# Three of four quads of gate/up as seven products, with one weight sum made by an adding transfer

## The chip, the cores and the metric

The kernel runs on one core of a Trainium2 chip. The metric is the device time of one execution in microseconds (us); the runs shown are three timed executions, and a separate profiled execution gives the trace.

## The reference

Two decoder layers over 256 tokens with 2048 features, all in float32. In each layer a mixer of two head groups (sparse attention with an indexer that picks 64 keys per query, and latent attention) is followed by a layer norm; then comes the part that this change is about:

```python
def _swiglu(x, w_gate, w_up, w_down):
    h = jax.nn.silu(jnp.einsum('bsd,df->bsf', x, w_gate)) * jnp.einsum('bsd,df->bsf', x, w_up)
    return jnp.einsum('bsf,fd->bsd', h, w_down)
...
        x = _layer_norm(ALPHA * x + mix, ln1_g[i], ln1_b[i])
        ffn = _swiglu(x, w_gate[i], w_up[i], w_down[i])
        x = _layer_norm(ALPHA * x + ffn, ln2_g[i], ln2_b[i])
```

The hidden width is 5632.

## The kernel before, in words

**Precision and units.** Every float32 operand of a large matmul is held as two parts, a rounded part (`xh`, `wh`) and the rest (`xl`, `wl`), and a product is three matmuls: high by high, high by low, low by high. Weights come in units: a DMA on the SP queue loads 512 KB into a `raw` tile (128 partitions by 2 k-tiles of 512 columns, line 302); `parts` makes `wh` from it on ScalarE (line 313) and `wl = raw - wh` on VectorE (line 314), both 1024 wide. This is called a split here. There are four `raw` slots, and two more in the phase "more", which holds the output projection's end and the feed-forward stage. For `wh` and `wl` there are five slots each (`UNITS`) and two more in that phase (`MORE`).

**Feed-forward stage.** The 5632 hidden columns are cut into eleven blocks (fc 0 to 10) of 512. A block computes gate and up for two token halves (128 tokens each): four sums over 16 k-tiles. Block 0 does this directly (`gu`). Blocks 1 to 10 (`gate_up`, line 863) treat it as 2 by 2 matrices: token half by contraction half on one side, contraction half by gate/up on the other. A *quad* is the four weight units w11 (gate, unit u), w21 (gate, unit u+4), w12 and w22 (up, the same units). A *plain* quad (`plain_quad`) multiplies all eight pairs. A *seven-product* quad (`wino_quad`, line 905) forms sums of the four weight tiles on VectorE (line 911, four of them, 1024 wide), splits the seven resulting operands, and multiplies them with the tokens or with sums of token tiles (`sum_operands`, kept in the tile `many`) in seven products, each into its own PSUM bank or added onto one of them. After the block's last seven-product quad the banks are recombined on VectorE into gate and up (lines 926 to 959); these statements stand under `tc.high_priority(offset=60)`, which moves them ahead of others that are ready.

The order of quads in each of blocks 1 to 10 is plain, seven-product, plain, seven-product (`ORDER`, line 1023). Behind a block, `hidden` (line 842) takes silu(gate) times up, and three units later transposes the result on PE (line 355) and splits it into `hT`.

**Down.** `down` (line 980) multiplies a pair of hidden blocks with `w_down` for given columns; a half is two of the four column groups, 8 units, 96 matmuls. From block 2 on, half a down pass runs behind the first quad of each block (`behind_quad`, line 1012). For the first pair of blocks VectorE adds it onto the residual `x`, scaled by ALPHA (line 991); for others ScalarE copies it out (line 994) and a DMA issued by GpSimd adds it onto `x` (line 995, `x<-d`, 256 KB). The second half of the last pair and block 10's own part (`last_pass`, line 778) come after block 10; then the last norm (`moments`, line 364, and `norm_out`) writes the output.

**Order.** A planner puts the instructions of each engine and DMA queue into one fixed order ahead of the run, by the program's order and by when it expects an instruction to be ready. An engine works through its order and waits where a value or a buffer isn't there yet.

Of the kernel before, what the change touches and what calls it, by code (L numbers as in the profile page):

```python
# [31 lines left out]
P = 128  # L32
D = 2048
# [23 lines left out]
UNITS, MORE = 5, 2  # L57
# [3 lines left out]
T2 = 11  # L61
# [17 lines left out]
def hybrid_trunk(ctx: ExitStack, tc: tile.TileContext, x, xt_in, pos, w_in, g_cq, g_ckv, w_uq,  # L79
# [34 lines left out]
    def t2(shape, s, dt=F32):  # L114
        return sb.tile(shape, dt, name=nm(s), tag="t2", bufs=T2)

# [70 lines left out]
    def rope_tables():  # L187
        n = NT * NF
        invf = const.tile([P, NF], F32, name="invf")
# [7 lines left out]
        a = const.tile([P, NT, NF], F32, name="ang")  # L197
# [3 lines left out]
        k = const.tile([P, n], F32, name="rk")  # L201
        kh = const.tile([P, n], F32, name="rkh")
# [31 lines left out]
        ab = const.tile([P, NT, NF], F32, name="absang")  # L234
# [86 lines left out]
    def proj(units, lhs, n, before=None, split_t=None):  # L321
# [3 lines left out]
        o = [acc() for _ in range(NT)]  # L325
# [38 lines left out]
    def moments(y):  # L364
# [8 lines left out]
        nc.gpsimd.tensor_scalar(ve, mv[:, 1:2], LN_EPS, None, ALU.add)  # L373
# [41 lines left out]
    def affine(g, b, c):  # L415

        sl = slice(c * C, (c + 1) * C)
        gc, bc = load_gb(g, b, sl)
        for t in range(NT):
            nc.vector.tensor_tensor(xt[t][:, sl], xt[t][:, sl], gc, op=ALU.mult)  # L420
            nc.vector.tensor_tensor(xt[t][:, sl], xt[t][:, sl], bc, op=ALU.add)

    def norm_out(t, gb, m):
        mu, rs = m
        nb = small([P, 1], "bnnb")
        nc.vector.scalar_tensor_tensor(nb, mu, -1.0, rs, op0=ALU.mult, op1=ALU.mult)
        for c in range(D // C):
            sl = slice(c * C, (c + 1) * C)
            y = xt[t][:, sl]
            if t and c == 0:  # L430
                nc.vector.tensor_scalar(y, y, mu, rs, ALU.subtract, ALU.mult)
            else:
                nc.scalar.activation(y, y, AF.Identity, bias=nb, scale=rs)
            nc.vector.tensor_tensor(y, y, gb[c][0], op=ALU.mult)
            (nc.vector if t and c != 1 else nc.gpsimd).tensor_tensor(y, y, gb[c][1], op=ALU.add)
            nc.sync.dma_start(out[t * P:(t + 1) * P, sl], y)
# [43 lines left out]
    def layer(l, xh, xl, norms, last):  # L480
# [297 lines left out]
        def last_pass(unit, ks, lhs, then):  # L778
# [6 lines left out]
            for t in range(NT):  # L785
                for c in range(D // C):
# [10 lines left out]
                    nc.vector.tensor_tensor(sl, sl, o, op=ALU.add)  # L797
# [22 lines left out]
        def sum_operands():  # L820


            for k0, n, where in ((4, 4, many([P, 4, 2, 4, P])),):
                a = {}
                for t in range(NT):
                    for i in range(2):
                        ks = slice(k0 + i * NKT // 2, k0 + i * NKT // 2 + n)
                        v = a[t, i] = t2([P, n, P], "av")
                        nc.vector.tensor_tensor(v, f(xh[t][:, ks, :]), f(xl[t][:, ks, :]), op=ALU.add)
                prev = {}  # L830
                for i, (x, y) in enumerate((((1, 0), (1, 1)), ((0, 0), "s1"), ((1, 0), (0, 0)), ((0, 1), "s2"))):
                    v = prev[f"s{i + 1}"] = t2([P, n, P], "sv")
                    nc.vector.tensor_tensor(v, a[x], prev[y] if isinstance(y, str) else a[y], op=ALU.subtract)
                    hi, lo = where[:, i, 0], where[:, i, 1]
                    split(hi, lo, v)
                    for k in range(n):
                        sums[f"s{i + 1}", k0 + k] = hi[:, k, :], lo[:, k, :]

# [3 lines left out]
        def hidden(gs, us, hT, tr):  # L842

            ss = []
            for t in range(NT):
                g, u = gs[t], us[t]
                s = t2([P, C], "silu")
                nc.scalar.activation(s, g, AF.Silu)
                nc.vector.tensor_tensor(s, s, u, op=ALU.mult)
                ss.append(s)  # L850
            yield 3
            for t in range(NT):
                tp = tr(t)
                transpose4([ss[t][:, j * P:(j + 1) * P] for j in range(4)], tp)
# [250 lines left out]
```

## Time and profile before

| | |
|---|---|
| runs shown | 2196.02, 2196.47, 2197.36 us (median 2196.47) |
| the profiled execution | 2193.86 us, of which its span is 2191.9 us |
| loads of w_gate, w_up, w_down | 176 each, 512 KB each |
| seven-product quads | 40 (160 weight sums on line 911) |
| adding transfers `x<-d` | 64 of 256 KB |

All times of the trace are counted from the start of the span. PE is TensorE's matmuls, PEld its weight loads, DVE is VectorE, ACT ScalarE, POOL GpSimd, SP the engine that issues the loads. In the groups of instructions a row has line, engine, operation, output and inputs with their shapes, count; then busy us in total, mean ns of one; then the engine's idle time before them and who ended it. In a timeline row the first number is the start, the second the duration; brackets give the idle time before it and its end's cause.

### The profile page before, as it was taken

How to read it: one execution, taken by the hardware profiler on the slowest of the kernel's cores; microseconds unless marked ns; L12 is line 12 of the kernel's file. 1: busy time of each engine (PE TensorE's matmuls, PEld its weight loads, DVE VectorE, ACT ScalarE, POOL GpSimd, SP SyncE). 2: the span in 40 equal slices, each digit the busy share in tenths (PEclk: the TensorE clock that was granted, in tenths of full speed). 3: DMA queues.
4: the chain of work that ended last, by engine and by line, in shares of the span. 5: the costliest groups of instructions: out<-in, count | busy, mean ns of one | idle time of the engine just before them, and what ended most of it. 6: DMA issues, size and time to landing. Idle time of an engine off the chain costs nothing. (4 is left out here: it accounts for less than half of the span.)

```text
span 2191.9 us, 27923 instructions
## 1 busy us (share of the span) xinstructions
PE 2169.4 (99%) x10128; PEld 1804.3 (82%) x10128; DVE 1709.0 (78%) x2223; ACT 1196.7 (55%) x1537; POOL 103.9 (5%) x198
## 2 busy tenths in 40 slices
PE   8999999999999999999999999999999999999997
PEld 7888888888888888888888888888888888888886
DVE  6685557989878888887857757678989778888876
ACT  5555554655555555555555554446555655555553
POOL 0100000100000000000001000000000000000012
PEclk9999999999999999999999999999999999999999
DMA  8554456556567667666745455555565667667674
GB/s 299 168 168 154 154 182 210 194 187 216 189 199 245 194 220 240 206 214 203 233 148 170 155 176 178 199 195 186 208 225 183 216 202 231 201 214 238 218 225 133
DMA packets 126058, 437.04 MB, mean 199 GB/s; under 512 B 14320, under 2 KB 14368, under 8 KB 125664
## 3 DMA queue, kind: packets, MB, share of 16 engines
q1 hardware_dynamic: 113760, 409.26, 55.2%
q0 software_dynamic: 12160, 26.01, 6.0%
q8 instruction: 79, 1.29, 0.2%
q14 instruction: 59, 0.48, 0.1%
HBM read 416.33 MB, written 2.10 MB: 191 GB/s over the span
## 5 line engine op out<-in xcount | busy, mean ns | idle before, releaser
L313 ACT ACTIVATE wh<-raw 128x1024 fp32r<-128x1024 f32 (+1 forms) x876 | 916.2, 1056 | 792.2 <-PE acc L337 350.4
L314 DVE TENSOR_TENSOR wl<-raw,wh 128x1024 fp32r<-128x1024 f32 (+1 forms) x876 | 1050.6, 1216 | 379.8 <-ACT wh L313 368.0
L335 PE MATMUL acc<-wh,xh 128*128 128x512 f32 (+1 forms) x768 | 303.4, 396 | 5.9 <-ACT wh L313 5.9
L337 PE MATMUL acc<-wh,xl 128*128 128x512 f32 (+1 forms) x768 | 298.1, 389 | 0.0
L336 PE MATMUL acc<-wl,xh 128*128 128x512 f32 (+1 forms) x768 | 297.5, 388 | 0.0
L335 PE MATMUL acc<-wh,hT 128*128 128x512 f32 x640 | 248.9, 389 | 1.6 <-DVE e L958 1.6
L336 PE MATMUL acc<-wl,hT 128*128 128x512 f32 x640 | 249.0, 389 | 0.0
L337 PE MATMUL acc<-wh,hT 128*128 128x512 f32 x640 | 248.8, 389 | 0.0
L911 DVE TENSOR_TENSOR raw<-raw,raw 128x1024 f32<-128x1024 f32 x160 | 195.7, 1224 | 21.9 <-DMA raw<-in_w_up_dram 17.9
L882 PE MATMUL gu_c<-wh,xl 128*128 128x512 f32 x480 | 186.7, 389 | 0.0
L879 PE MATMUL gu_c<-wh,xh 128*128 128x512 f32 x480 | 186.7, 389 | 0.0
L881 PE MATMUL gu_c<-wl,xh 128*128 128x512 f32 x480 | 186.7, 389 | 0.0
L335 PEld LDWEIGHTS acc<-wh,xh 128*128 128x128 f32 x768 | 144.9, 189 | 36.9 <-ACT wh L313 6.6
L337 PEld LDWEIGHTS acc<-wh,xl 128*128 128x128 f32 x768 | 144.8, 188 | 29.0 <-DVE xl L401 1.0
L336 PEld LDWEIGHTS acc<-wl,xh 128*128 128x128 f32 x768 | 145.1, 189 | 27.6 <-DVE wl L314 1.8
L335 PEld LDWEIGHTS acc<-wh,hT 128*128 128x128 f32 x640 | 120.1, 188 | 27.0 <-DVE e L958 2.0
L337 PEld LDWEIGHTS acc<-wh,hT 128*128 128x128 f32 x640 | 120.1, 188 | 24.9
L336 PEld LDWEIGHTS acc<-wl,hT 128*128 128x128 f32 x640 | 120.2, 188 | 24.8
L879 PE MATMUL att<-wh,xh 128*128 128x512 f32 x320 | 126.1, 394 | 0.0
L882 PE MATMUL att<-wh,xl 128*128 128x512 f32 x320 | 124.9, 390 | 0.0
L881 PE MATMUL att<-wl,xh 128*128 128x512 f32 x320 | 124.6, 389 | 0.0
L995 POOL DMA_DIRECT2D x<-d x64 | 55.1, 879 | 1202.0 <-ACT d L994 697.0
(269 smaller groups left out, 3067.9 us busy)
## 6 DMA issues: line engine op xcount, KB each, us to landing
raw<-in_w_gate_dram SPq DMA_DIRECT2D x176, 512.0 KB, 5.1
raw<-in_w_up_dram SPq DMA_DIRECT2D x176, 512.0 KB, 4.7
raw<-in_w_down_dram SPq DMA_DIRECT2D x176, 512.0 KB, 4.5
raw<-in_w_in_dram SPq DMA_DIRECT2D x144, 512.0 KB, 3.7
raw<-in_w_o_dram SPq DMA_DIRECT2D x64, 512.0 KB, 4.0
x<-d POOLq DMA_DIRECT2D x64, 256.0 KB, 5.8
raw<-in_w_in_dram SPq DMA_DIRECT2D x16, 400.0 KB, 3.1
raw<-in_w_uq_dram SPq DMA_DIRECT2D x12, 512.0 KB, 3.3
```

The source lines that it names most:

```text
L313: nc.scalar.activation(wh[:, :n], raw[:, :n], AF.Copy)
L314: nc.vector.tensor_tensor(wl[:, :n], raw[:, :n], f(wh[:, :n]), op=ALU.subtract)
L335: mm(o[t][:, :n], h, a, start=first, stop=False)
L336: mm(o[t][:, :n], h, b, start=False, stop=False)
L337: mm(o[t][:, :n], l, a, start=False, stop=final)
L879: mm(o[name], h, a, start=name not in begun, stop=False)
L881: mm(o[name], h, b, start=False, stop=False)
L882: mm(o[name], l, a, start=False, stop=end)
L911: nc.vector.tensor_tensor(d, x, y, op=ADD)
L995: nc.gpsimd.dma_start(sl, d, accum_op=ALU.add)
```

## The change

- Blocks 3 to 10 take three of their four quads as seven products, in the order seven-product (unit 1), seven-product (2), plain (0), seven-product (3). Block 1 has three plain quads and one seven-product quad, block 2 keeps two and two. Token sums for unit 1 are added (`few`).
- From block 3 on, the half down pass runs ahead of the block's first quad, and the transposes of the hidden block ahead of it come after eight units, behind that half. The down pass of the last pair is done whole after block 10.
- In a seven-product quad the sum w12 + w22 is made by a DMA: w12 is loaded, and a transfer issued by GpSimd adds w22 onto it from memory; w22 is loaded by itself too. The order of products is p1, p2, p6, p7, p4, p5, p3, and VectorE makes three sums.
- Gate and up, and the two recombined halves, lie in one tile each for both token halves, so that p5, the up bank pair and the product with silu(gate) are each one operation of 1024 for both.
- `MORE` goes from 2 to 3. The temporaries `t2` go from 11 to 5, with 6 more in the attention phase; the rope tables use one of them.
- All down parts go through ScalarE and the adding DMA; ALPHA is put into the gains and offsets of the norm ahead (`affine`, scaled on ScalarE).
- The last norm uses whole gain and offset tiles (three of 1 MB, loaded once gate/up has left their slots); its epsilon step is on VectorE, two of its columns have the offset added by a DMA onto it, no addition is on GpSimd, and the last column is stored in two halves. The additions onto `x` in the last pass are put ahead by 200 (`SOON`).

```diff
-UNITS, MORE = 5, 2
+UNITS, MORE = 5, 3
+SOON = 200
+FIRSTD = 3
-T2 = 11
+T2, T2MORE = 5, 6
...
-        nc.gpsimd.tensor_scalar(ve, mv[:, 1:2], LN_EPS, None, ALU.add)
+        nc.vector.tensor_scalar(ve, mv[:, 1:2], LN_EPS, None, ALU.add)
...
+    def gains():
+
+        g, b, b2 = (t8([P, D], F32, s) for s in ("gall", "ball", "ball"))
+        for d, v in ((g, ln2_g), (b, ln2_b), (b2, ln2_b)):
+            nc.gpsimd.dma_start(d, v[DEPTH - 1].partition_broadcast(P))
+        return g, b, b2
...
             if t and c == 0:
-                nc.vector.tensor_scalar(y, y, mu, rs, ALU.subtract, ALU.mult)
-            else:
-                nc.scalar.activation(y, y, AF.Identity, bias=nb, scale=rs)
-            nc.vector.tensor_tensor(y, y, gb[c][0], op=ALU.mult)
-            (nc.vector if t and c != 1 else nc.gpsimd).tensor_tensor(y, y, gb[c][1], op=ALU.add)
-            nc.sync.dma_start(out[t * P:(t + 1) * P, sl], y)
+                nc.vector.scalar_tensor_tensor(y, y, mu, g[:, sl], op0=ALU.subtract, op1=ALU.mult)
+                nc.vector.scalar_tensor_tensor(y, y, rs, b[:, sl], op0=ALU.mult, op1=ALU.add)
+                store(y, c * C, C)
+                continue
+            nc.scalar.activation(y, y, AF.Identity, bias=nb, scale=rs)
+            nc.vector.tensor_tensor(y, y, g[:, sl], op=ALU.mult)
+            if not t and c < 2:
+                nc.gpsimd.dma_start(b2[:, sl], y, accum_op=ALU.add)
+                late.append(c)
+                continue
+            halves = 2 if t and c == D // C - 1 else 1
...
-            for k0, n, where in ((4, 4, many([P, 4, 2, 4, P])),):
+            few = t8([P, 4, 2, 2, P], F32R, "few")
+            for k0, n, where in ((4, 4, many([P, 4, 2, 4, P])), (2, 2, few)):
...
             def wino_quad(u, final):
-                r11, r21, r12, r22 = (load_raw(w_gu[i][l, fc, v], KU * C) for i, v in
-                                      ((0, u), (0, u + HALF), (1, u), (1, u + HALF)))
+                r12 = load_raw(w_gu[1][l, fc, u], KU * C)
+                nc.gpsimd.dma_start(r12, w_gu[1][l, fc, u + HALF], accum_op=ADD)
+                r11, r21, r22 = (load_raw(w_gu[i][l, fc, v], KU * C) for i, v in ((0, u), (0, u + HALF), (1, u + HALF)))
...
                 p("p2", token(0), r21, hi_)
...
-                add(r11, r11, r12)
-                p("p5", slhs("s1"), r11, lo_)
-                add(r12, r12, r22)
-                add(r11, r11, r22)
+                nc.vector.tensor_tensor(r11, r12, r11, op=ADD)
                 p("p6", slhs("s2"), r11, lo_)
                 if final:
-                    with sooner():
-                        nc.vector.tensor_tensor(e, o["p6"], e, op=ALU.subtract)
+                    on(e[:, 0, :], o["p6"], e[:, 0, :], SUB)
+                nc.vector.tensor_tensor(r21, r11, r21, op=ADD)
+                p("p7", slhs("s3"), r12, lo_)
+                if final:
+                    on(e[:, 1, :], e[:, 0, :], o["p7"], ADD)
                 tick()
-                p("p7", slhs("s3"), r12, lo_)
-                add(r21, r11, r21)
...
                 p("p4", token(1), r21, hi_)
                 if final:
-                    with sooner():
-                        g1 = t2([P, C], "g1")
-                        nc.vector.tensor_tensor(g1, o["c21"], v, op=ALU.subtract)
+                    on(g[:, 1, :], o["c21"], e[:, 1, :], SUB)
+                nc.vector.tensor_tensor(r11, r11, r22, op=SUB)
+                p("p5", slhs("s1"), r11, lo_)
+                if final:
+                    on(e, e, o["p5"].unsqueeze(1).to_broadcast([P, NT, C]), ADD)
                 tick()
                 p("p3", slhs("s4"), r22, lo_)
                 if final:
-                    nc.vector.tensor_tensor(v, v, o["p5"], op=ADD)
-                    nc.vector.tensor_tensor(v, v, o["c22"], op=ADD)
-                    nc.vector.tensor_tensor(e, e, o["p5"], op=ADD)
-                    nc.vector.tensor_tensor(e, e, o["c12"], op=ADD)
+                    on(e, e, o["up"], ADD)
...
                 for t in range(NT):
-                    sl = xt[t][:, c * C:(c + 1) * C]
-                    if fcs[0] == 0:
-                        nc.vector.scalar_tensor_tensor(sl, sl, ALPHA, o[t], op0=ALU.mult, op1=ALU.add)
-                    else:
-                        d = t2([P, C], "d")
-                        nc.scalar.activation(d, o[t], AF.Copy)
-                        nc.gpsimd.dma_start(sl, d, accum_op=ALU.add)
+                    d = t2([P, C], "d")
+                    nc.scalar.activation(d, o[t], AF.Copy)
+                    nc.gpsimd.dma_start(xt[t][:, c * C:(c + 1) * C], d, accum_op=ALU.add)
...
-        ORDER = [("plain", 0), ("wino", 2), ("plain", 1), ("wino", 3)]
+        ORDER = {1: "NNNS", 2: "NSNS"}
+        UNIT = {"NNNS": (0, 1, 2, 3), "NSNS": (0, 2, 1, 3), "SSNS": (1, 2, 0, 3)}
...
         for fc in range(1, NFC):
-            g, u = gate_up(fc, ORDER, behind_quad(fc))
+            order = ORDER.get(fc, "SSNS")
+            if fc >= FIRSTD:
+                down_half(fc)
+                finish_hidden()
+            g, u = gate_up(fc, [({"N": "plain", "S": "wino"}[k], v) for k, v in zip(order, UNIT[order])],
+                           finish_hidden if fc < FIRSTD else None)
...
-        down(held[:2], (2, 3))
+        down(held[:2], range(D // C))
```

More of the change, by code (lines that the diff above doesn't have):

```diff
@@ L319, in load_unit, with proj @@
         return parts(load_raw(src, n), n)
-    def proj(units, lhs, n, before=None, split_t=None):
-        o = [acc() for _ in range(NT)]
+    def proj(units, lhs, n, before=None, split_t=None, banks=None):
+        o = [bank(i, "acc") for i in banks] if banks else [acc() for _ in range(NT)]
         loaded = []
@@ L421, in affine, with store @@
             nc.vector.tensor_tensor(xt[t][:, sl], xt[t][:, sl], bc, op=ALU.add)
+    def gains():
[3 more added lines that the diff above has]
+        return g, b, b2
     def norm_out(t, gb, m):
         mu, rs = m
+        g, b, b2 = gb
         nb = small([P, 1], "bnnb")
         nc.vector.scalar_tensor_tensor(nb, mu, -1.0, rs, op0=ALU.mult, op1=ALU.mult)
+        def store(v, c0, n, queue=nc.sync):
+            queue.dma_start(out[t * P:(t + 1) * P, c0:c0 + n], v)
+        late = []
         for c in range(D // C):
@@ L796, in last_pass @@
                     sl = xt[t][:, c * C:(c + 1) * C]
-                    nc.vector.tensor_tensor(sl, sl, o, op=ALU.add)
+                    with tc.high_priority(offset=SOON):
+                        nc.vector.tensor_tensor(sl, sl, o, op=ALU.add)
                 then(t)
@@ L969, in gate_up @@
                     r = wino_quad(u, i == len(order) - 1)
-                if i == 0:
+                if i == 0 and between:
                     between()
@@ L1003, in layer, with spawn_hidden @@
         held = []
-        def spawn_hidden(fc, g, u, tr):
+        def spawn_hidden(fc, g, u):
             hT = t8([P, 2, 4, S], F32R, "hT")
-            held.append((fc, hT, spawn(hidden(g, u, hT, tr))))
-        def free_banks(t):
-            return bank(2 + t, "tr")
-        def behind_quad(fc):
-            def go():
-                if fc < 2:
-                    return finish(*[h[2] for h in held])
-                down(held[:2], (0, 1) if fc % 2 == 0 else (2, 3))
-                if fc % 2:
-                    del held[:2]
-                finish(*[h[2] for h in held])
-            return go
@@ L1023, in layer, with down_half, finish_hidden @@
-        ORDER = [("plain", 0), ("wino", 2), ("plain", 1), ("wino", 3)]
+            wait = 3 if fc + 1 < FIRSTD else 8 if fc + 1 < NFC else 6
+            held.append((fc, hT, spawn(hidden(g, u, hT, wait))))
+        def down_half(fc):
+            down(held[:2], (0, 1) if fc % 2 else (2, 3))
+            if fc % 2 == 0:
+                del held[:2]
+        def finish_hidden():
+            finish(*[h[2] for h in held])
+        ORDER = {1: "NNNS", 2: "NSNS"}
+        UNIT = {"NNNS": (0, 1, 2, 3), "NSNS": (0, 2, 1, 3), "SSNS": (1, 2, 0, 3)}
@@ L1037, in layer @@
         xh, xl, norms, ms = [], [], [], []
         if last:
-            gb = [load_gb(ln2_g[l], ln2_b[l], slice(c * C, (c + 1) * C)) for c in range(D // C)]
+            gb = gains()
         else:
             gbT = load_gbT(ln2_T[l])
-        down(held[:2], (2, 3))
+        down(held[:2], range(D // C))
         finish(held[2][2])
+        turns["acc"] = 1
         u0 = C // P // KU * (NFC - 1)
```

121 lines of the change are left out of this document (67 added, 54 removed).

## The prediction

> **What bounds the kernel now.** I read the page first (engine totals, clock), then the busy time by stage, then each engine's timeline inside one repeating feed-forward block, then the DMA rows and the last 15 us.
>
> ```profile
> span 2191.9 us, 27923 instructions
> PE 2169.4 (99%) x10128; PEld 1804.3 (82%) x10128; DVE 1709.0 (78%) x2223; ACT 1196.7 (55%) x1537; POOL 103.9 (5%) x198
> PEclk9999999999999999999999999999999999999999
> 1696.50:1759.96 63.46, 63.46 (x286) 52.65 (x285) 52.18 (x51) 36.21 (x39) 3.49 (x4) 1.00 0.68 216
> 2077.26:2142.58 65.32, 63.75 (x286) 52.57 (x285) 52.01 (x51) 36.68 (x40) 7.78 (x12) 1.00 0.75 237
> ```
>
> The first three lines are the page's: TensorE is busy 99% of the span at full clock. The last two are the stage view, for one block (from one pair of hidden transposes to the next) and for the last block: length, then busy time of PE, weight load, DVE, ACT and POOL, the clock, the DMA share, GB/s. In the ordinary block PE is never idle, and VectorE works 52.18 of 63.46 us. A busy PE need not run at its peak, so I checked the pace in the timeline:
>
> ```profile
> 1636.48 0.39 PE L335 MATMUL acc<-wh,hT 128*128 128x512 f32 x1
> ...
> 1658.02 0.39 PE L337 MATMUL acc<-wh,hT 128*128 128x512 f32 x1
> ```
>
> These are the first and the last of the 96 matmuls of one down half: (1658.02 - 1636.48)/95 = 0.2267 us each, though one lasts 0.39. A block has 180 gate/up and 96 down matmuls: 276 x 0.2267 = 62.57 us, and the eight transposes are the other 0.89 of 63.46. So the time of a block is its count of matmuls, and that count is what this change cuts, if the other engines still deliver.
>
> **The change, part by part.**
>
> *Matmuls.* A plain quad is 48 matmuls (2 outputs x 2 token halves x 2 units x 2 k-tiles x 3 passes), a seven-product quad is 7 x 2 x 3 = 42. Blocks 3 to 10 go from two to three such quads, block 1 from two to one, block 2 keeps two: per layer 8 x 6 - 6 = 42 fewer, in two layers 84. 84 x 0.2267 = 19.0 us off PE. A block becomes 270 x 0.2267 + 0.89 = 62.1 us.
>
> *VectorE and ScalarE in a block.*
>
> ```profile
> L314 DVE TENSOR_TENSOR wl<-raw,wh 128x1024 fp32r<-128x1024 f32 x860 | 1034.7, 1221 | 360.8 <-ACT wh L313 349.3
> L313 ACT ACTIVATE wh<-raw 128x1024 fp32r<-128x1024 f32 x860 | 902.2, 1059 | 771.0 <-PE acc L337 329.2 <-DVE raw L911 126.1 <-issue 62.4
> L911 DVE TENSOR_TENSOR raw<-raw,raw 128x1024 f32<-128x1024 f32 x160 | 195.7, 1224 | 21.9 <-DMA raw<-in_w_up_dram 17.9
> 1733.03 1.22 DVE L314 TENSOR_TENSOR wl<-raw,wh 128x1024 fp32r<-128x1024 f32 x1
> 1734.17 1.22 DVE L911 TENSOR_TENSOR raw<-raw,raw 128x1024 f32<-128x1024 f32 x1
> 1753.17 0.68 DVE L956 TENSOR_TENSOR v<-v,gu_p 128x512 f32<-128x512 f32 x1
> 1753.77 0.68 DVE L958 TENSOR_TENSOR e<-e,gu_p 128x512 f32<-128x512 f32 x1
> ```
>
> Starts 1733.03 and 1734.17 give 1.14 us per 1024-wide operation back to back; 1753.17 and 1753.77 give 0.60 per 512-wide one. Splits go from 30 to 33 per block. Weight sums on VectorE go from 2 x 4 to 3 x 3, because the fourth of each quad is now the adding transfer: 4 more operations, 4 x 1.14 = 4.6 us. Recombining goes from ten 512-wide operations (6.0) to four of these and three joined 1024-wide ones (5.8); no row has the joined form with a PSUM operand or a repeated one, so I bound it by 1.14 (as SBUF sums) and 1.20 (two halves): no difference that counts. VectorE: 52.2 + 4.6 - 0.2 = 56.6 of 62.1 us, 91%. ScalarE adds three copies, 3.2 us, to 36.2: far from a limit. Neither is a bound by its total.
>
> But VectorE is loaded unevenly. A seven-product quad costs it (7 + 3) x 1.14 = 11.4 us against 42 x 0.2267 = 9.5 on PE, so the two at the front of a block lose 2 x 1.9 = 3.8 us against PE, with 1.2 more for splitting the hidden block. The cover is the down half ahead of them (21.8 us on PE, 9.1 in splits), which lets it run ahead up to eight prepared units, about seven products of 1.36 us, or 9.5 us. That covers 5.0. Were the cover gone, 5.0 x 16 blocks = 80 us.
>
> *The adding transfer.* The load of w12 goes out on SP, GpSimd waits for it and then adds w22 onto it (w22 is also loaded by itself, so this is traffic on top); the first VectorE sum of the quad waits for that, behind this wait on VectorE stand all later splits, and behind them PE.
>
> ```profile
> DMA to landing us min/median/max: 3.3/5.8/10.0
> DMA to landing us min/median/max: 3.2/4.8/6.3
> q1 hardware_dynamic: 3457, 12.59, 58.2%
> q0 software_dynamic: 576, 1.05, 9.3%
> ```
>
> The first row is of the 64 adding transfers x<-d (256 KB, SBUF to SBUF, line 995), the second of the block's 24 weight loads (512 KB, line 302), the others the block's two DMA queues. Four x<-d take 9.3% of 63.46 us, 1.48 us of all sixteen engines each, where a load of twice the size takes 36.9/24 = 1.54. No row shows an adding transfer of 512 KB from memory. From below it is bounded by a plain load, 3.2; otherwise I add 1.48 us to the x<-d row for the second 256 KB: 4.8, 7.3 or 11.5 us. I take 7.3, nearest in kind.
>
> The first two quads of a block have time: their raw slots come free before or early in the down half. The third is the tight one. Clock 0 at the block's first down matmul: PE ends the down half at 21.8, the transposes at 22.7, quad one at 32.2, two at 41.7, the plain one at 52.6, three at 62.1. The raw slots that quad three loads into come free as quad two's products are split, in the worst case with its sixth. VectorE can begin on quad two at about 22.9 (the last down unit leaves its slot at 21.8, plus a 1.06 us copy) and has by then two hidden splits (1.2) and ten 1024-wide operations (11.4) to do: 35.5. Issue 0.3, load 4.8, GpSimd's issue 0.9 (3.49 us of POOL for four x<-d in the block): 41.5. At the other end, VectorE has after the sum eight 1024-wide operations and four 512-wide ones, 11.5 us, and must be done as PE gets to the last product, 62.1 - 1.36 = 60.7: the sum must be there by 49.2. That leaves the transfer 7.7 us. With 7.3 it is in time by 0.4; with 4.8 by 2.9; with 11.5 PE waits 3.8 us in each block. If the slot comes free with the fifth product the margin is some 3 us larger. I charge 2 us in all, for a few blocks with a slow load (6.3).
>
> The Trainium skill, *DMA: Bandwidth & Descriptors*, section "Anatomy of one DMA — SWDGE (gpsimd) path", fits such a transfer as 2.0 us plus bytes over 436 GB/s; estimated by it 256 KB take 2.6 us and 512 KB 3.2, the sum would never be late and the 2 us would not be charged. The x<-d row speaks against it here: 5.8 us in the middle and not one under 3.3.
>
> *Queues.* The down half passes the block's first quad: its 8 loads on SP, 4 copies on ScalarE and 4 x<-d on GpSimd now stand ahead of it. GpSimd issues 7 instead of 4 transfers per block, 6 us of 62. The order on a queue is not the program's:
>
> ```profile
> 1740.20 0.33 SPq L302 DMA_DIRECT2D raw<-in_w_up_dram  x1
> 1741.34 0.33 SPq L302 DMA_DIRECT2D raw<-in_w_down_dram  x1
> 1742.47 0.33 SPq L302 DMA_DIRECT2D raw<-in_w_up_dram  x1
> ```
>
> A w_down load stands between two w_up loads that the program puts ahead of it, so a ready transfer passes one whose buffer isn't; I take it that the sum transfers pass x<-d that still wait for PE. The DMA share becomes (0.68 x 63.46 + 3 x 2.96)/62.1 = 84%, so loads land a little later; that is in the 2 us.
>
> *Blocks 0 to 2.* The first two pairs of half sums become x<-d (ScalarE 8 x 0.6 us more, VectorE as much less), the scaled gains cost ScalarE eight copies a layer, and the second set of token sums twelve VectorE operations of some 0.4 us, 5 us a layer. Against them blocks 1 and 2 have three splits and seven sums fewer than now (11.4 us).
>
> ```profile
> L994 ACT ACTIVATE d<-acc 128x512 f32<-128x512 f32 x64 | 38.0, 597 | 32.0 <-PE acc L337 31.9
> L359 DVE TENSOR_TENSOR xl<-xs,xh 128x256 fp32r<-128x256 f32 x16 | 6.0, 418 | 3.1 <-ACT xh L358 3.1
> 116.97 0.44 PE L355 MATMUL tr<-ident,rn 128*128 128x128 f32 x2 [0.99 <-ACT kpT L524]
> ```
>
> PE has no gap there now, and VectorE gets lighter by 6 us a layer: 0. Temporaries fall from 11 to 5 outside attention, where the recombining no longer uses them; a down column needs two in 10.9 us, each held 0.6 + 0.9 + 5.8 us. I price that at 0; a wait would cost about what the last row shows, 0.99 us, PE's gap in the first layer's attention.
>
> *The last block and the end.*
>
> ```profile
> 2137.28 0.50 PE L335 MATMUL acc<-wh,hT 128*128 128x512 f32 x1 [1.57 <-DVE e L958]
> 2107.78 10.23 DMA raw<-in_w_up_dram
> 2105.21 0.86 POOL L411 DMA_DIRECT2D g<-in_ln_g_dram  x1
> 2180.32 0.28 DVE bnmv L370
> 2180.67 0.23 POOL bnve L373
> 2181.65 0.54 DVE L431 TENSOR_SCALAR x<-x,bnmv,bnrs 128x512 f32<-128x512 f32 x1
> 2186.32 1.28 DVE L435 TENSOR_TENSOR x<-x,b 128x512 f32<-128x512 f32 x2
> L434 DVE TENSOR_TENSOR x<-x,g x8: 678/692/1750, 2171.7 to 2185.7; 128x512 f32<-128x512 f32 x8
> ```
>
> PE's one stall in the feed-forward stage, 1.57 us, follows a weight load of 10.23 us that shared the engines with the gain loads issued from 2104 on. The new gain tiles take big slots that come free only when gate/up ends, so their 3 MB fall beside the last down pass (192 matmuls, 43.5 us on PE, 18 in splits, six raw slots ahead): -1.6; without that cover the 1.57 comes back. At the end VectorE works from 2181.65 to 2187.60, 5.95 us; now the first column is two operations (1.2), the next two are two each (2.4), the last is one and two halves (1.3): 4.9. With epsilon added on VectorE, not by a GpSimd step of 0.23, I take -1.2 together, between 0 and -2.
>
> Part of the 5.95 are the slow ones among line 434's products, 1750 ns for 678, in the stretch where GpSimd's additions run; those are gone.
>
> Sum against the profiled execution (2193.86, span 2191.9 and 1.96 around it): -19.0 - 1.6 - 1.2 + 2.0 = -19.8, 2174.1. That execution lies 2.6 under the median of the runs, 2196.47, so the median becomes **2176.7**.
>
> **The rivals.**
>
> *The third quad's sum is late in every block (slower).* It takes 8 to 10 us rather than 7.3, or load and transfer are both slow in the fuller DMA. For it: the 10.0 us maximum of x<-d, a margin of 0.4, a DMA share going from 68% to 84%. Against: the median, and the larger margin in the other slot order. 0.2% of this kernel is 4.4 us, about what its measurement can tell from no change. It is slower by that once PE waits (21.8 + 4.4)/16 = 1.6 us per block, so from a transfer of 9.3 us on; at 11.5, 3.8 x 16 = 61, 2236.
>
> *The sum is late in part.* With one layer's slot order, or now and then: 0.5 to 1 us in each block, 8 to 16 us, 2183 to 2191.
>
> *VectorE's lead doesn't last.* If it enters the two front quads with half its lead, 4.8 us for the 5.0, and waits 1 us there for a sum, PE loses 1.2 us a block, 19 us: 2196, no change. Against it: 5.5 us of VectorE are free in each block.
>
> *The change doesn't do what it says:* the planner puts a front quad's transfer behind the four x<-d, the last of which waits for the end of the down half. Then it starts at 23.5, lands at 31.7, is split by 35.1 where PE needs it at 25.4: 9.7 x 16 = 155, 2330. The SP rows speak against it.
>
> **How the numbers follow.** Full saving 0.57 (2171 to 2182); late in part 0.18 (2182 to 2191); lead lost 0.08 (2192 to 2200); late throughout 0.13 (2201 to 2240), misplaced 0.04. Low end 2171: nothing late (-2.0), the end at its bound (-0.8), and the 2.6 by which execution and median differ. High end 2197, within the lead case: about 0.2 is left out. Faster 0.75, same 0.08, slower 0.17.
>
> **What would show it.** Right: 84 matmuls fewer; block length 62.1 with PE idle under 0.2; VectorE 56 to 57 in it; no PE wait behind a split in the third quad; 162 VectorE sums on weights (54 quads x 3) and 54 adding transfers of 512 KB. Wrong: blocks over 63 us, waits of the first sum on an adding transfer that reach PE, transfers that land after 9 us, or a GpSimd queue where x<-d stands ahead of a front quad's sum.

## The result, and the profile after

The changed kernel takes 2224.93 us, the median of 4 runs (2221.38 to 2229.4), against 2196.24 us (2193.48 to 2197.36) for 4 runs of the kernel before on the same chip: a ratio of 1.0134, 95% interval 1.0113 to 1.0154. It is 1.3% slower where 0.9% faster was forecast. The profiled execution took 2224.56 us, with a span of 2222.8.

First the page of the changed kernel, its totals, the clock and the queue of GpSimd's transfers:

```profile
span 2222.8 us, 28085 instructions
PE 2169.5 (98%) x10044; PEld 1787.7 (80%) x10044; DVE 1739.8 (78%) x2226; ACT 1233.2 (55%) x1619; POOL 154.4 (7%) x252
PEclk9999999999999999999999999999999999999999
q0 software_dynamic: 22320, 60.09, 14.1%
```

TensorE has 84 matmuls fewer, as meant, and is busy as long as before (the same matmuls take 2147.5 us in `no_sum` below, so part of the loss lies inside the busy time). 2222.8 - 2169.5 = 53 us of the span it now stands idle, 22.5 before. The mean granted clock is 0.996, against 0.998 before. The groups of instructions say whom it waits for (last column: idle time just before these instructions, and who ended it), and who waits itself:

```profile
L339 PE MATMUL acc<-wh,hT 128*128 128x512 f32 x640 | 252.9, 395 | 18.9 <-DVE e L961 16.6 <-ACT wh L317 1.9
L923 PE MATMUL gu_p<-wl,many 128*128 128x512 f32 x228 | 90.8, 398 | 9.2 <-DVE wl L318 9.1
L975 DVE TENSOR_TENSOR raw<-raw,raw 128x1024 f32<-128x1024 f32 x54 | 66.1, 1223 | 94.9 <-DMA raw<-in_w_up_dram 94.9
```

The first weight sum of the seven-product quads (line 975) waits 94.9 us for the adding transfers, all of its idle time. The 54 transfers themselves, and the 80 into the residual stream, in the list of DMA issues (KB each, median us to landing):

```profile
raw<-in_w_up_dram POOLq DMA_DIRECT2D x54, 512.0 KB, 8.1
x<-d POOLq DMA_DIRECT2D x80, 256.0 KB, 7.8
```

and the spread of the 54, by the view of line 951:

```profile
DMA to landing us min/median/max: 5.1/8.1/10.7
```

Now one block late in the second layer, from transposes to transposes: the stage view (the columns as before),

```profile
1971.08:2036.18 65.10, 63.23 (x279) 51.20 (x278) 55.15 (x52) 37.44 (x43) 6.03 (x7) 1.00 0.77 228
```

and what VectorE waited for in it (us in total, times, longest):

```profile
DVE raw L975 <- DMA raw<-in_w_up_dram: 7.0, 2, 4.9
DVE wl L318 <- ACT wh L317: 2.7, 3, 1.3
```

The block lasts 65.10 us, not 62.1. VectorE's work and its waits fill it: 55.15 + 7.0 + 2.7 = 64.85. They nearly fill every block, late or not, since VectorE takes its instructions in order and either works or waits (a block of `no_sum` below, from 602.18 on: 55.98 and 5.8); which wait costs time is for the experiments to say. In the chain of waits through this block (start, duration, what), the way to the last quad's sum:

```profile
1984.17 4.75 DMA raw<-in_w_up_dram
1988.99 0.51 issue
1989.50 10.20 DMA raw<-in_w_up_dram
```

The timeline of GpSimd, with this transfer's issue and those of the next block's two front quads:

```profile
1989.50 0.85 POOL L951 DMA_DIRECT2D raw<-in_w_up_dram  x1 [15.88 <-DMA raw<-in_w_up_dram]
...
2020.30 0.85 POOL L951 DMA_DIRECT2D raw<-in_w_up_dram  x1 [29.95 <-DMA raw<-in_w_up_dram]
2032.70 0.85 POOL L951 DMA_DIRECT2D raw<-in_w_up_dram  x1 [11.55 <-DVE raw L979]
2033.24 2.06 POOL L1026 DMA_DIRECT2D x<-d  x2
```

The timelines of PE, around the two ends of the block, and of VectorE behind the wait:

```profile
1948.91 0.47 PE L339 MATMUL acc<-wh,hT 128*128 128x512 f32 x1 [0.83 <-DVE e L961]
...
2011.78 0.39 PE L924 MATMUL att<-wh,many 128*128 128x512 f32 x1
2014.00 0.47 PE L339 MATMUL acc<-wh,hT 128*128 128x512 f32 x1 [1.83 <-DVE e L961]
```

```profile
1999.79 1.23 DVE L975 TENSOR_TENSOR raw<-raw,raw 128x1024 f32<-128x1024 f32 x1 [4.89 <-DMA raw<-in_w_up_dram]
2000.93 3.49 DVE L318 TENSOR_TENSOR wl<-raw,wh 128x1024 fp32r<-128x1024 f32 x3
...
2006.74 4.78 DVE L318 TENSOR_TENSOR wl<-raw,wh 128x1024 fp32r<-128x1024 f32 x4
2011.44 0.68 DVE L961 TENSOR_TENSOR g<-e,gu_c 128x512 f32<-128x512 f32 x1
```

Read on the prediction's clock, whose 0 is the block's first down matmul (1948.91): the load of w12 goes out at 35.3, lands at 40.0, GpSimd issues at 40.6, the sum can start at 50.8. VectorE stands idle for 4.89 us before it. In this block PE gets through the block's last product with no gap (2011.78) and then waits 1.83 us, at the first matmul of the next down half, for a recombining operation of VectorE. Over the whole run PE waits in two ways, by its two groups above: 16.6 us at the down matmuls for VectorE's recombining, and 9.1 us at products, behind splits, nearly all of that in the first layer.

### The profile page after: what moved, and what is told of

Its sections match the earlier page's. It is cut to its first block, busy times and chain, and to the rows that moved or that the text cites. A ratio compares the mean times of both kernels' runs of the same rounds, so it can differ in the third digit from the quotient of the medians.

```text
span 2222.8 us, 28085 instructions
## 1 busy us (share of the span) xinstructions
PE 2169.5 (98%) x10044; PEld 1787.7 (80%) x10044; DVE 1739.8 (78%) x2226; ACT 1233.2 (55%) x1619; POOL 154.4 (7%) x252
## 3 DMA queue, kind: packets, MB, share of 16 engines
q0 software_dynamic: 22320, 60.09, 14.1%
## 5 line engine op out<-in xcount | busy, mean ns | idle before, releaser
L317 ACT ACTIVATE wh<-raw 128x1024 fp32r<-128x1024 f32 (+1 forms) x918 | 944.0, 1053 | 809.5 <-PE acc L341 213.3
L318 DVE TENSOR_TENSOR wl<-raw,wh 128x1024 fp32r<-128x1024 f32 (+1 forms) x918 | 1093.5, 1217 | 292.7 <-ACT wh L317 289.6
L339 PE MATMUL acc<-wh,hT 128*128 128x512 f32 x640 | 252.9, 395 | 18.9 <-DVE e L961 16.6
L923 PE MATMUL gu_c<-wl,xh 128*128 128x512 f32 x424 | 165.4, 390 | 0.3 <-DVE wl L318 0.3
L921 PE MATMUL gu_c<-wh,xh 128*128 128x512 f32 x424 | 165.0, 389 | 0.0
L924 PE MATMUL gu_c<-wh,xl 128*128 128x512 f32 x424 | 165.0, 389 | 0.0
L975 DVE TENSOR_TENSOR raw<-raw,raw 128x1024 f32<-128x1024 f32 x54 | 66.1, 1223 | 94.9 <-DMA raw<-in_w_up_dram 94.9
L951 POOL DMA_DIRECT2D raw<-in_w_up_dram x54 | 46.1, 853 | 988.8 <-DMA raw<-in_w_up_dram 435.9
L923 PE MATMUL gu_p<-wl,many 128*128 128x512 f32 x228 | 90.8, 398 | 9.2 <-DVE wl L318 9.1
L923 PEld LDWEIGHTS gu_c<-wl,xh 128*128 128x128 f32 x424 | 79.6, 188 | 18.4 <-DVE wl L318 1.9
L921 PEld LDWEIGHTS gu_c<-wh,xh 128*128 128x128 f32 x424 | 79.6, 188 | 16.6
```

Of the source, the lines that this page charges most:

```text
L317: nc.scalar.activation(wh[:, :n], raw[:, :n], AF.Copy)
L318: nc.vector.tensor_tensor(wl[:, :n], raw[:, :n], f(wh[:, :n]), op=ALU.subtract)
L339: mm(o[t][:, :n], h, a, start=first, stop=False)
L921: mm(o[name], h, a, start=name not in begun, stop=False)
L923: mm(o[name], h, b, start=False, stop=False)
L924: mm(o[name], l, a, start=False, stop=end)
```

## The experiments

Three theories stand at the start. **A, the late sum:** the last quad's adding transfer lands too late, VectorE waits for it in order, and at 91% load cannot make that up. **B, VectorE itself:** its load, uneven over the block, is too much, whoever makes the fourth sum. **C, added traffic:** 28 MB of further reads (54 x 512 KB) slow all weight loads. The kernel before ran beside each version: medians of 2195.5 to 2195.9 us.

### Which of the three

`no_sum` takes the transfer away; it leaves out the addition of w22 to w12.

```
                 r12 = load_raw(w_gu[1][l, fc, u], KU * C)
-                nc.gpsimd.dma_start(r12, w_gu[1][l, fc, u + HALF], accum_op=ADD)
```

> Leaves out part of the computation: w22 is not added onto w12 in any seven-product quad; the adding transfers are gone, nothing takes their place. Theory A (the third quad's sum arrives late: raw slot, load, GpSimd's issue and a transfer of about 9 us in a row, VectorE stands 4.3 us in each of 16 blocks at its first sum, and at 91% load it can't make that up before PE gets there): the waits go, blocks take about 62.2, 2175 to 2182. Theory B (VectorE's own load, 33 splits, 9 sums and the recombining that the down half's first banks wait for, is too much or too uneven whatever the sum does): VectorE's work is the same, so blocks stay at 65 and the time at 2215 to 2228. Theory C (the 28 MB of added traffic make all loads late): traffic is back to before, 2175 to 2185, like A.

Measured: 2172.4 us, ratio 0.9898 (0.9881 to 0.9914), span 2169.2. The stage view of a block:

```profile
540.06:602.18 62.12, 62.12 (x279) 51.53 (x278) 55.95 (x51) 38.09 (x42) 3.37 (x5) 1.00 0.73 219
```

The block has the 62.1 us that the count of matmuls gives, with VectorE at the same work (55.95) and PE never idle. So all that was lost, 2222.8 - 2169.2 = 53.6 us of span, comes from the transfer, and B is out: with this load on VectorE, nothing else late, PE keeps its pace. A and C both stand. What VectorE waits for in a block is here almost only ScalarE, 3.9 us for copies of weights and 1.5 for the hidden block (the block from 602.18 on); in the late block above that had shrunk to 2.7. So VectorE's waits give way to one another, up to a point.

`own_sum` makes the fourth sum on VectorE, as the other three, from the loaded w22:

```
-                nc.gpsimd.dma_start(r12, w_gu[1][l, fc, u + HALF], accum_op=ADD)
...
+                nc.vector.tensor_tensor(r12, r12, r22, op=ADD)
```

> Only the adding transfer is undone: w12 + w22 is a fourth VectorE sum in every quad, order of quads, down half first and joined recombining as in the changed kernel. VectorE gets 3 x 1.14 = 3.4 us more per block, 60 of 62.1, 96%. Theory A: no wait on a transfer is left, but little slack either; PE waits perhaps 0.5 to 1 us a block: 2182 to 2196, below the changed kernel by 30 or more. Theory B: 3.4 x 16 = 54 us on top of 2225, 2260 to 2285. Theory C: 2175 to 2185.

Measured: 2201.11 us, ratio 1.0026 (1.0016 to 1.0036). All three missed. B is refuted by its size, but VectorE does start to bind: in the stretch from 600 to 1040 us it works 403.31 of 440 us (391.40 in `no_sum`). One operation more per quad is 3 x 1.14 = 3.4 us per block. PE now waits for splits here and there, but from 600 to 2100 us most for ScalarE's copies of the down sums (line 1025); why ScalarE is late there was not followed. Stage view, timeline, and PE's longest wait in that stretch (us in total, times, longest):

```profile
600.00:1040.00 440.00, 431.63 (x1907) 353.54 (x1906) 403.31 (x369) 260.07 (x290) 22.21 (x26) 1.00 0.68 211
```

```profile
582.37 0.50 PE L923 MATMUL gu_p<-wl,many 128*128 128x512 f32 x1 [1.25 <-DVE wl L318]
```

```profile
PE gu_p L921 <- ACT d L1025: 8.7, 9, 2.4
```

`third_own` keeps the transfer in the two front quads and makes the last quad's sum on VectorE:

```
+                if not final:
                     nc.gpsimd.dma_start(r12, w_gu[1][l, fc, u + HALF], accum_op=ADD)
...
+                if final:
+                    nc.vector.tensor_tensor(r12, r12, r22, op=ADD)
```

> The adding transfer stays in the two quads at the front of a block; in a block's last seven-product quad VectorE makes the fourth sum. VectorE 1.14 us more per block, 57.7 of 62.1. Theory A: the one sum that was late is gone, 2176 to 2188, and VectorE's wait at a first sum is under 2 us a block. Theory B: 1.14 x 16 = 18 more, 2240 to 2246. Theory C: 27 to 30 of 54 added transfers stay, so half to two thirds of the loss of 48 us stays: 2200 to 2212.

Measured: 2184.12 us, ratio 0.9959 (0.9943 to 0.9975). As A has it: 34 of the 54 transfers remain, and with those of the last quads 2224.93 - 2184.12 = 41 us are gone.

`hoist` keeps every operation and every byte, and only puts the last quad's load of w12 and its adding transfer ahead of the plain quad's loads, one quad earlier:

```
+            early = {}
+            def load_sum(u):
+                r = load_raw(w_gu[1][l, fc, u], KU * C)
+                nc.gpsimd.dma_start(r, w_gu[1][l, fc, u + HALF], accum_op=ALU.add)
+                return r
...
-                r12 = load_raw(w_gu[1][l, fc, u], KU * C)
-                nc.gpsimd.dma_start(r12, w_gu[1][l, fc, u + HALF], accum_op=ADD)
+                r12 = early.pop(u) if u in early else load_sum(u)
...
                 if kind == "plain":
+                    if fc >= FIRSTD:
+                        v = order[i + 1][1]
+                        early[v] = load_sum(v)
                     plain_quad(u, i == 0, i == lastp)
```

> The load of w12 and the adding transfer of a block's third seven-product quad are put ahead of the four loads of the plain quad before it; same work, same traffic. Theory A: it takes the raw slot that comes free first, 3 to 4 us earlier, so VectorE's wait of 4.3 us falls to 0 to 1.5 and the time to 2180 to 2200; if a plain quad's load is late instead, up to 2210. Theory B: nothing moves, 2222 to 2228. Theory C: nothing moves, 2222 to 2228.

Measured: 2177.76 us, ratio 0.9921 (0.9906 to 0.9936). A block of it:

```profile
1931.72:1993.85 62.13, 62.13 (x279) 51.52 (x278) 54.95 (x51) 38.21 (x42) 6.03 (x8) 1.00 0.80 240
```

and the spread of its 54 transfers:

```profile
DMA to landing us min/median/max: 5.1/5.4/10.3
```

This parts A from C: the same bytes, even a larger DMA share (0.80 for 0.77), and the block is back at 62.13. What C can be worth is the rest, 2177.76 - 2172.4 = 5.4 us at most. In the middle the 54 transfers land in 5.4 us, for 8.1. The sixteen that were moved (blocks 3 to 10 of both layers) take 5.3 in the middle, 5.1 to 7.1 in all, with the add; at their old place, in the changed kernel, the same sixteen took 9.1, 7.0 to 10.7.

### Which link of the chain

`raw8` gives the loads eight raw buffers for six and pays with one of the eight prepared units:

```
-UNITS, MORE = 5, 3
-RAWMORE = 2
+UNITS, MORE = 5, 2
+RAWMORE = 4
```

> Eight raw buffers instead of six and seven prepared units instead of eight. Late sum: the chain begins with the release of a raw buffer, two splits earlier it is released 2 to 5 us earlier, and the sum of the third quad is there before 49.2 on the block's clock: 2178 to 2200. If the third quad's transfer only gets into a fuller DMA by that, or if VectorE needs all eight prepared units of lead for the two front quads: 2205 to 2235.

Measured: 2186.23 us, ratio 0.996 (0.9948 to 0.9973). The sums' waits are gone, by the groups, and in PE's timeline two new ones are there:

```profile
L975 DVE TENSOR_TENSOR raw<-raw,raw 128x1024 f32<-128x1024 f32 x54 | 65.9, 1220 | 3.1 <-DMA raw<-in_w_up_dram 2.9
```

```profile
1043.91 0.79 PE L339 MATMUL acc<-wh,hT 128*128 128x512 f32 x1 [5.11 <-DVE hT L363]
2127.54 0.79 PE L339 MATMUL acc<-wh,hT 128*128 128x512 f32 x1 [3.84 <-DVE hT L363]
```

So the first link, the release of the raw buffer, is one handle: the transfers still take 7.5 us in the middle, but start early enough. The blocks of both layers have 62.1 us up to the last; the 5.11 + 3.84 = 9.0 us of the two rows, at the end of each layer's feed-forward stage, are about what separates it from `hoist` (8.5). That they come from the missing prepared unit was not tried by itself.

`plain_second` keeps the transfer in its place but lets it load w22 over w12; it leaves out the sum w12 + w22.

```
-                nc.gpsimd.dma_start(r12, w_gu[1][l, fc, u + HALF], accum_op=ADD)
+                nc.gpsimd.dma_start(r12, w_gu[1][l, fc, u + HALF])
```

> The transfer from GpSimd's queue no longer adds: it loads w22 over w12 (the sum w12+w22 is left out). Buffers, order, queues and bytes read stay. If the time of the transfer is that of a 512 KB transfer from this queue behind other loads, it still takes 7 to 9 us in the third quad and the kernel stays at 2210 to 2228. If it is the adding that makes it long, it takes 3 to 6 us as the plain loads do, the sum is in time and the kernel takes 2175 to 2195.

Measured: 2176.83 us, ratio 0.9915 (0.9899 to 0.9931): at this place it is the adding that makes the sum late; the queue and the bytes without it do not. Its 54 transfers by the view of their line, its queue on the page, a block in the stage view, and VectorE's waits in that:

```profile
DMA to landing us min/median/max: 3.6/5.8/8.8
```

```profile
q0 software_dynamic: 22320, 60.09, 10.9%
```

```profile
1933.93:1996.03 62.10, 62.10 (x280) 51.52 (x278) 55.71 (x51) 38.35 (x42) 5.07 (x8) 1.00 0.78 251
```

```profile
DVE wl L318 <- ACT wh L317: 3.0, 3, 1.5
DVE raw L975 <- DMA raw<-in_w_up_dram: 1.6, 1, 1.6
```

The same packets and megabytes take 10.9% of sixteen engines' span, for 14.1% with the add. Per transfer, above the 7.2% of `no_sum`'s queue, and taking the rest of the queue to cost the same in all three: (14.1% x 2222.8 - 7.2% x 2169.2)/54 = 2.9 us of all sixteen engines with the add, (10.9% x 2177.2 - 7.2% x 2169.2)/54 = 1.5 without. In the middle the add costs 8.1 - 5.8 = 2.3 us to landing at this place (for the sixteen last quads 9.1 and 7.2), and that is enough; 0.3 of it is GpSimd's issue, 0.85 us with the add and 0.54 without. It is not a price of the add alone: in `hoist` the sixteen moved transfers add and land in 5.3.

`p3_third` takes P3, which needs no weight sum, third instead of last in the last quad, so that the sum is needed one product later:

```
                 p("p2", token(0), r21, hi_)
...
+                if final:
+                    p("p3", slhs("s4"), r22, lo_)
...
                     on(g[:, 1, :], o["c21"], e[:, 1, :], SUB)
+                    on(e, e, o["up"], ADD)
...
-                p("p3", slhs("s4"), r22, lo_)
-                if final:
-                    on(e, e, o["up"], ADD)
+                if not final:
+                    p("p3", slhs("s4"), r22, lo_)
```

> In the third seven-product quad the product P3, which needs no weight sum, is taken third instead of seventh, and its 1024-wide recombining operation goes ahead of P5; transfers, sums and matmuls stay. Late sum: the first sum is needed one product (1.36 us) and one split later, and the split of w22 no longer has to come after it, so most of the 3 us that each block loses is saved: 2180 to 2200. VectorE's load or the added memory traffic as the cause: neither changes, 2218 to 2230.

Measured: 2243.01 us, ratio 1.021 (1.0182 to 1.0237): a miss for every theory as I had put it. VectorE waits somewhat less for the transfers (79.2 us in all), PE much more, and nearly all at one place: 39.7 us at down matmuls for a recombining operation (16.6 in the changed kernel), 0.9 at products behind splits. The timeline of PE at the end of block 2, of VectorE there, and the stage view in steps of 4 us around it (the column after POOL's is the granted clock):

```profile
522.16 0.47 PE L339 MATMUL acc<-wh,hT 128*128 128x512 f32 x1 [2.40 <-DVE e L961]
526.24 0.80 PE L339 MATMUL acc<-wh,hT 128*128 128x512 f32 x1 [2.29 <-DVE e L961]
```

```profile
524.36 1.23 DVE L318 TENSOR_TENSOR wl<-raw,wh 128x1024 fp32r<-128x1024 f32 x1 [2.34 <-ACT wh L317]
525.50 0.68 DVE L961 TENSOR_TENSOR e<-e,gu_p 128x512 f32<-128x512 f32 x1
```

```profile
522.00:526.00 4.00, 1.78 (x6) 1.05 (x6) 1.66 (x3) 2.73 (x3) 0.00 (x0) 0.68 0.98 383
526.00:530.00 4.00, 3.76 (x9) 3.00 (x10) 4.00 (x5) 3.38 (x5) 0.85 (x1) 0.50 0.82 228
530.00:534.00 4.00, 4.00 (x19) 3.22 (x18) 4.00 (x5) 1.37 (x2) 0.00 (x0) 0.96 1.02 231
```

Here the lateness is not felt at a product. It is felt at the next down half, whose first column writes the two PSUM banks that hold P6 and P7 until VectorE has recombined them. With P3 moved forward, two products stand between P7 and that point instead of three, so PE gets there 1.36 us sooner. VectorE does not: in its order splits stand between the recombining operations, and the one before the second gap's end waits 2.34 us for ScalarE. After the first gap the granted clock falls to half for some microseconds: nine matmuls in 4 us where nineteen follow. The mean clock of this execution is 0.991, 0.996 for the changed kernel, 0.999 for `no_sum`.

### When a wait costs time

`nsns` keeps everything of the change but the third seven-product quad: blocks 3 to 10 run plain, seven, plain, seven, as before.

```
-            order = ORDER.get(fc, "SSNS")
+            order = ORDER.get(fc, "NSNS")
```

> Blocks 3 to 10 keep their two seven-product quads as before the change (plain, seven, plain, seven), everything else of the change stays: 96 matmuls more than after it, 12 more than before it (+2.7 us), and VectorE busy some 50 of 63.5 us per block. If a late sum costs time only because VectorE, at 91%, has nothing to make it up with: 2188 to 2200. If the late sum of the last quad costs its 3 us per block whatever VectorE's load: 2225 to 2245. If the changes outside the order of the quads cost time of their own: above 2205 with no wait for a sum in PE's idle time.

Measured: 2197.48 us, ratio 1.001 (1.0 to 1.002). The group of the first sums, one block of the first layer in the stage view, and VectorE's waits in it:

```profile
L975 DVE TENSOR_TENSOR raw<-raw,raw 128x1024 f32<-128x1024 f32 x38 | 46.5, 1224 | 113.3 <-DMA raw<-in_w_up_dram 113.0
```

```profile
671.13:734.58 63.45, 63.45 (x285) 52.65 (x284) 48.97 (x45) 35.29 (x39) 5.18 (x6) 1.00 0.78 233
```

```profile
DVE raw L975 <- DMA raw<-in_w_up_dram: 11.4, 2, 5.9
DVE wl L318 <- ACT wh L317: 2.2, 2, 1.5
```

The sums wait longer than in the changed kernel, 113.0 us, and it costs nothing: with 11.4 us of such waits the block has the 63.46 us of before. VectorE works 48.97 us of it and has 14.5 to wait in. So a wait of VectorE has no price of its own. Whether a sum that misses its own deadline would be free too, this run does not show: on the block's clock the first sum of its last quad starts at 42.1 to 49.0 us in blocks 3 to 10, and a block is 1.4 us longer than in the changed order.

`third_plain` asks whether it is then all waits that count, or the last quad's alone: only the last quad's transfer no longer adds (the sum w12 + w22 is left out there).

```
+                if final:
+                    nc.gpsimd.dma_start(r12, w_gu[1][l, fc, u + HALF])
+                else:
                     nc.gpsimd.dma_start(r12, w_gu[1][l, fc, u + HALF], accum_op=ADD)
```

> Only the last quad's transfer no longer adds (the sum w12+w22 is left out there); in the front quads it still adds. Where only the last quad's own margin counts, its transfer is shorter by as much as with all of them plain, and the kernel takes 2173 to 2182. Where VectorE's whole idle time per block counts (62.1 less 55.7 of work is 6.4 us), its wait of about 1.3 us on the first front quad's sum stays, so blocks come to 62.1 to 63.5: 2180 to 2200.

Measured: 2193.53 us, ratio 0.9992 (0.9983 to 1.0001), with blocks 3 to 9 of the second layer at 62.1 us and those of the first up to 67.0. The waits at the last quads' sums are those of `plain_second`, 39 us for 37 in blocks 3 to 10; those at the first front quads' sums are 20 us for 2. So the front quads matter too, but not by their waits as such: the second layer has 11 of the 20 us, and its blocks 3 to 9 lose nothing. In the first layer the last quad is late again.

To see when, take the start of the last quad's first sum on each block's own clock, in blocks 3 to 10, from the traces of the versions with this order of quads and of products (the middle of eight blocks), with what line 975 (or its like) waited in all for the transfers:

| version | sum starts, first layer | second layer | waits on transfers, us | span, us |
|---|---|---|---|---|
| changed kernel | 52.6 | 50.2 | 94.9 | 2222.8 |
| `third_plain` | 51.4 | 46.3 | 61.1 | 2193.8 |
| `plain_second` | 48.4 | 45.2 | 41.1 | 2177.2 |
| `hoist` | 43.3 | 45.8 | 35.8 | 2177.2 |
| `raw8` | 46.8 | 47.2 | 2.9 | 2184.6 |
| `hoist_all` (below) | 42.6 | 45.3 | 21.3 | 2171.3 |
| `no_sum` | 42.3 | 43.7 | 0 | 2169.2 |

These are 112 blocks. Of the 78 whose sum starts before 48.0, all but three take 62.1 us from one down half to the next. All 24 whose sum starts after 49.2, the prediction's deadline, take longer, by 0.3 to 6.3 us. So it is a deadline that counts, not the total of waits: the 31 us that `hoist` waits at front quads cost next to nothing, and `raw8`'s span has its two other waits in it. (The profiled execution of `hoist_all` was the fastest of its five.) That the front quads' waits hold VectorE up, and with it the release of the raw buffer for the last quad's load, fits these rows and was not tried by itself.

### A better version

`hoist_all` moves load and transfer ahead in blocks 1 and 2 as well.

```
-                    if fc >= FIRSTD:
+                    if i + 1 < len(order) and order[i + 1][0] == "wino":
```

> As the version with the last quad's load and adding transfer ahead of the plain quad, now in blocks 1 and 2 too. Late sum: the 2.4 us of waits that were left around the end of block 2 go, 2173 to 2178; if they come from something else, no change from 2178; if the early raw buffers take those of the plain quad's loads there, 2180 to 2186.

Measured: 2178.95 us (2173.13 to 2181.54), ratio 0.9925 (0.9911 to 0.9938). The waits in PE around block 2 are gone from the trace, but the times of `hoist` and of this one cannot be told apart, so what was expected of those waits is neither shown nor refuted. Both beat the kernel before by 0.8% and the changed one by 2.1%.

## Why the prediction was wrong

**What held.** 84 matmuls fewer, 54 transfers, 162 sums on VectorE (three groups of 54). Blocks of 62.1 us at 0.2267 us per matmul wherever the sum is in time (`no_sum`, `hoist`, `plain_second`). VectorE at 55 to 56 us per block there, forecast 56.6. GpSimd's order: at 2020.30 and 2032.70 the front quads' sums go out ahead of the x<-d of 2033.24. The last block's stall is gone where the sum is in time, and the stretch behind PE's last matmul is 1.7 us shorter (forecast 1.2). The whole of the change but for the late sum is the span of `no_sum`: 2169.2 - 2191.9 = -22.7, forecast -19.0 - 1.6 - 1.2 = -21.8. The deadline of 49.2 held, as the table of the seven versions shows. The DMA share came out below the forecast: 0.77 in the late block, 0.80 in `hoist`, for 0.84.

**The step that failed** is the chain that ends with the last quad's sum: "With 7.3 it is in time by 0.4". In the changed kernel, blocks 3 to 10 (the middle of eight, in brackets the smallest and the largest; us on the block's clock, the transfer from the start of GpSimd's issue):

| | forecast | first layer | second layer |
|---|---|---|---|
| load of w12 goes out | 35.5 | 38.6 (36.7 to 40.2) | 35.0 (33.1 to 36.7) |
| GpSimd issues the transfer | 40.6 | 44.3 (42.3 to 46.1) | 40.5 (38.2 to 41.9) |
| the transfer | 0.9 + 7.3 | 7.5 (7.0 to 10.7) | 9.4 (8.9 to 10.2) |
| the sum starts | 48.8, needed by 49.2 | 52.6 (49.8 to 53.8) | 50.2 (47.7 to 51.3) |
| to the next down half | 62.1 | 66.2 (62.8 to 68.4) | 64.5 (62.1 to 65.6) |

Two terms of it were wrong, one in each layer. In the second layer it is the size of the adding transfer: "I take 7.3, nearest in kind". The row it was built on counts from the start of GpSimd's issue, so the issue's 0.9 stood in the sum twice, and even so 9.4 is more than 8.2. It rested on x<-d in a kernel where those were the only adding transfers and the DMA was 68% busy. The term added for the second 256 KB was right: twice 1.48 = 2.96 us of all sixteen engines, measured 2.9. What I did not add is that this load falls on neighbours that were already in the sum: x<-d itself went from 6.2 in `no_sum` to 7.8 (5.8 before the change).

In the first layer, which lost more, the transfer was no longer than forecast and the start was late: "VectorE can begin on quad two at about 22.9" and is through its sixth split by 35.5. The load waits for a split of VectorE to free its buffer, and that came 3 us later, at 38.6. Part of this is the transfers again: in `plain_second` the load goes out at 35.0 to 36.7 in the first layer and at 32.7 in the second. So at quad two VectorE was not where I had it; the block shown above, with 35.3 and 40.6, agrees with the forecast, but it is one of the second layer.

The margin of 0.4 us was far less than what I knew of that time, from 4.8 to 11.5, and the 2 us that I charged price the middle of that range, not its upper half. No run shows the 2 us as such: the sixteen blocks together lost 47 us against 62.1 each.

The Trainium skill, *DMA: Bandwidth & Descriptors*, section "Anatomy of one DMA — SWDGE (gpsimd) path", fits 2.0 us plus bytes over 436 GB/s, 3.2 us for 512 KB as an estimate. Of the plain transfers from that queue the fastest took 3.6 us, in the middle they took 5.8; with the add none took under 5.1. In this busy kernel the fit is a floor.

**The price of lateness** was in part too low. I had it as PE's loss, one for one. Beyond 49.2 the sums of the sixteen blocks are 34 us late in all, so one for one accounts for 34 of the 47 us. In the block shown 1.7 us late cost 3.0. The remaining 13 us were not followed; among them is the clock, which fell to half for 3.4 us in one of these blocks (below).

**The rivals.** "The third quad's sum is late in every block" is what happened in 13 of the 16 blocks, given 0.13; the measured median lies in its range. Its condition, a transfer from 9.3 us on, is met by the block shown (10.20 - 0.85 = 9.35 behind the issue), but not in the middle of either layer (8.5 and 6.6 behind it): the late start did the rest. "VectorE's lead doesn't last" has a part in it, by the late start in the first layer. "Misplaced" was false. That the excess is lateness and not a slower DMA as such is shown by `hoist`.

**Open.** How much of the longer landing is the add in the sixteen engines and how much the neighbouring loads is not parted; between `plain_second` and the changed kernel both differ. In `third_plain` the plain transfers of the last quads landed in 7.3 us in the middle, not in 5.8, though they did not add; but in `plain_second` too those of the last quads took 7.2, so the place counts. Why the first layer's loads go out later than the second's, in `plain_second` as well, was not followed (the prediction had allowed for two slot orders, some 3 us apart). That the two PSUM banks are what makes PE wait at the down half is read from the traces of the changed kernel and `p3_third`; other banks were not tried.

## What to carry to other kernels

Taking work off the busiest engine brings its count times its pace only if the next engine still delivers in time. Its waits cost nothing by themselves (113 us of them in `nsns` did not); put each operation that it must wait for on the stage's clock, against the time by which it is needed, and do so for every layer, since one block need not speak for all. An operation that an in-order engine must wait for is best issued a stage early, which here turned 1.3% slower into 0.8% faster with no other change. Where a margin is smaller than the spread of the one duration it rests on, the late case deserves as much weight as the other.

## What the hardware showed that I had not expected

The add in a DMA is not free. 512 KB from memory onto a tile take 2.9 us of all sixteen engines with the add and 1.5 as a plain transfer from the same queue, by the shares worked out above. To landing it is 9.1 and 7.2 us in the last quads, and 5.3 with the add where `hoist` puts it.

Short gaps can cost twice. In the changed kernel a single gap of 1.81 us was followed by 3.4 us at half the granted clock; in the timeline of PE, and in the stage view:

```profile
1821.97 0.47 PE L339 MATMUL acc<-wh,hT 128*128 128x512 f32 x1 [1.81 <-DVE e L961]
```

```profile
1822.60:1826.00 3.40, 3.40 (x10) 2.61 (x9) 3.40 (x5) 2.96 (x4) 0.00 (x0) 0.51 1.03 399
```

The same followed the gap of 1.89 us before 118.30, while that of 1.83 us in the block shown left the clock at 1.00: not every gap of this length does it, and what decides is not shown. In `p3_third` the clock was at half from 523.5 on, after the first gap of 2.40 us and before the second. The Trainium skill, *TensorE: Matmul & The Clock Gate*, section "HAM oscillation — how this bites in real kernels", warns of idle gaps of more than about 3.4 us; here single gaps of 1.81 and 1.89 us were enough.
